# Norm sums as columns of tokens, and two merge groups moved behind the attention drain, in a kernel of two nets

## The chip, the cores and the metric

The kernel runs on 1 core of one Trainium2 chip. The metric is the device time of one execution in microseconds (us). The engines are named as the profile names them: PE (TensorE, matrix products), PEld (its weight loads), DVE (VectorE), ACT (ScalarE), POOL (GpSimd) and SP (SyncE, which here only issues transfers).

## The reference, cut to what matters

Two nets run one after the other on 512 tokens of 1024 channels in fp32. Each has two layers.

```
# first net, each of DEPTH = 2 layers
h = rms_norm(x, g_mix[l]);  proj = h @ w_in[l]
y_a, y_b, y_c = mla_mixer(...), dilated_mixer(...), neighbourhood_mixer(...)
gates = sigmoid(gate_logits)
merged = gates[0]*(y_a @ w_pa[l]) + gates[1]*(y_b @ w_pb[l]) + gates[2]*(y_c @ w_pc[l])
x = x + merged @ w_o[l]
x = x + (silu(rms_norm(x, g_ffn[l]) @ w1[l]) * (rms_norm(x, g_ffn[l]) @ w3[l])) @ w2[l]
...
x = rms_norm(x, g_final)
# second net, each of 2 layers
h = layer_norm(x) * (1 + scale) + shift          # scale, shift, gate from c @ w_ada[l] + b_ada[l]
proj = h @ w_in[l]
y = [attention | short convolution | fourier], each times silu(gate)
x = layer_norm(alpha * x + gate * (y @ w_out[l])) * ln_g[l] + ln_b[l]
```

## The kernel before

Channels lie on partitions: an activation is 8 tiles of 128 channels x 512 tokens. An fp32 product is made of three matmuls of halves (`mm3`, L267 to L271): hi x hi (L269), lo x hi (L270), hi x lo (L271). `weights` (L257 to L264) loads a weight tile `wst` by a transfer that SP issues; ACT makes its high half `whi` (L251), DVE its low half `wlo` (L252). A scheduler orders the instructions of each engine before the run, and each engine then goes through its own list in that order. SP's list holds nearly all weight loads and the loads and stores of `td`, a buffer in HBM. PSUM has banks named mm (3), S (2), O (1) and T (2).

**First net.** `branches` runs the groups of the attentions (scores L341, exponentials on ACT, transposes L365, value products L406, and the division at the end, L415 to L417 and L506 to L508) and weaves "fill" between them: products of the gates and of the branches that stand ready. The last stretch of fill is `first_products`: for each n of 8 a "merge group" of 42 matmuls, namely the gate of branch a (24), y_a @ w_pa (12, weights `wpa`) and y_b @ w_pb (6, weights `wpb`); the sum goes to `td[n]`. When the fill is used up, the last two attention groups still have to finish: that stretch is called the drain below. Behind it stands the loop over w_pc (12 matmuls for each n, which go to the banks S, T, O, mm by turns; it loads `td[16+n]` into a tile O and `td[n]` into a tile tmp), then the loop over w_o. The product y_c needs all of the last attention groups for its last two k-tiles of 128 only.

**Second net.** The work before it and between its layers has three passages in which a norm over channels stands between two stretches of matrix products. A sum over channels is a matmul of a 128x128 tile of ones with a 128x512 tile (`add_sum`, L1105), which gives the sum of all tokens on every partition:
- A, `centre` (L1107 to L1156): both norms (rms of the first net, layer norm of the second). POOL adds up the tiles for n < 7, and the sums of tile 7 are added on PE; `fold` (L1090) sums the modulation on PE in matmuls of one column; the square root is taken on ACT (L1176) and the reciprocal on DVE on 128x512 (L1185); then `less_mean` and `put_h` (L1266, L1267) make the input hh of the next products.
- B, between the layers (L1478 to the end of `second_layer`): POOL adds up x and its square (L1494, L1495), DVE x times the gain (L1489); then 5 sums, a pass over the 8 tiles (L1546 to L1550, 16 sums on PE), a fold, a reciprocal and `put_h`.
- C, the last norm (L1500 to L1533): the sums, then subtraction, a reciprocal in two halves, scaling and 8 output transfers.

Of the kernel before, what the change touches and what calls it, by code (L numbers as in the profile page):

```python
# [19 lines left out]
D = 1024  # L20
# [194 lines left out]
class _Net:  # L215
# [357 lines left out]
    def first_layer(self, l, acc, xsrc, emit_x):  # L573
        nc, a = self.nc, self.a
        with ExitStack() as lctx:
# [45 lines left out]
            def first_products(early):  # L621

                yh, yl = ys["a"]
                bh, bl = ([x[:, i] for i in range(2)] for x in (qk_tiles(), qk_tiles()))
                put = [load_split(4 + i, bh[i], bl[i]) for i in range(2)]
                yield from gates(len(todo))
                for f in put:
                    f()
                for n in range(8):
                    if n == 6:  # L630
                        early()
                    t = self.t(self.tp, "gate", (P, S), bufs=2)
                    yield from gate(0, n, t)
                    w = self.weights(a["wpa"][l, n])
                    pz = self.bank("mm")
                    for i in range(4):
                        o = slice(i * P, i * P + P)
                        self.mm3(pz, w[0][:, o], w[1][:, o], yh[:, i], yl[i], i == 0, i == 3)
                        yield 650
                    nc.vector.scalar_tensor_tensor(t, t, 1.0, pz, op0=ALU.add, op1=ALU.mult)  # L640
                    t1 = self.t(self.tp, "E", (P, S), bufs=3)
                    nc.sync.dma_start(out=t1, in_=td[8 + n])
                    w = self.weights(a["wpb"][l, n])
                    pz = self.bank("mm")
                    yield from self.dense_steps(pz, w, (bh, bl), range(2))
                    nc.vector.scalar_tensor_tensor(t1, t1, 1.0, pz, op0=ALU.add, op1=ALU.mult)
                    nc.gpsimd.tensor_tensor(t, t, t1, op=ALU.add)
                    nc.sync.dma_start(out=td[n], in_=t)
                    yield 0

            with ExitStack() as actx:
# [4 lines left out]
                              first_products, load_split, qk_tiles, qc)  # L656

# [115 lines left out]
    def branches(self, l, r, put_r, gates, first_outputs, first_products, load_split, qk_tiles, qc):  # L773
# [279 lines left out]
        fills[6] += 8 * 9100  # L1053
# [52 lines left out]

    def centre(self, n, x, state):  # L1107
# [21 lines left out]
        if 0 < n < 7:  # L1129
            for k, y in (("d", d), ("x", sq), ("q", dq)):  # L1130
                nc.gpsimd.tensor_tensor(state[k], state[k], y, op=ALU.add)
        if n == 6:
            self.pm, self.pv, self.px = (self.bank(t) for t in "SOT")
            self.add_sum(self.px, state["x"], True, False)
            self.add_sum(self.pm, state["d"], True, False)
            self.add_sum(self.pv, state["q"], True, False)
            self.root_table(sq)
        if n == 7:
            self.add_sum(self.px, sq, False, True)
            self.add_sum(self.pm, d, False, True)  # L1140
            at = self.add_sum(self.pv, dq, False, True)
            pg = self.bank("mm")
# [4 lines left out]
            m2, q = (self.t(self.tp, t, (P, S), bufs=2) for t in ("s", "xo"))  # L1147
            r = self.scale = self.fp.tile([P, S], F32, name="scale")
            nc.scalar.activation(m2, self.pm, AF.Square, scale=1.0 / D)
            nc.scalar.activation(self.mean, self.pm, AF.Copy, scale=1.0 / D)  # L1150
            nc.vector.tensor_scalar(q, self.px, 1.0 / D, EPS, op0=ALU.mult, op1=ALU.add)
            nc.vector.scalar_tensor_tensor(m2, q, LN_EPS, m2, op0=ALU.mult, op1=ALU.subtract)
# [59 lines left out]
    def second_net(self):  # L1212
        nc, a, tc = self.nc, self.a, self.tc
        with ExitStack() as ctx:
# [8 lines left out]
            sd = self.t(self.tp, "tmp", (P, S))  # L1223
            nc.scalar.activation(sd, self.px, AF.Sqrt, scale=1.0 / D, bias=self.eps)
            nc.vector.reciprocal(self.r0, sd)
# [18 lines left out]
            self.gb = cp.tile([P, 8], F32, name="gb")  # L1244
            nc.vector.tensor_tensor(self.gb, self.col("ln_g0", 0, 8), self.bcol, op=ALU.mult)
            b2 = self.t(cp, "rq", (P, 8), bufs=2)
            nc.vector.tensor_tensor(b2, self.bcol, self.bcol, op=ALU.mult)
            pb = self.bank("ms")
            nc.tensor.matmul(pb[:, 0:8], self.onef, b2, start=True, stop=True)
            self.bvar = cp.tile([P, 1], F32, name="bvar")  # L1250
            nc.vector.tensor_reduce(self.bvar, pb[:, 0:8], axis=AX.X, op=ALU.add)
            nc.vector.tensor_scalar(self.bvar, self.bvar, 1.0 / D, LN_EPS, op0=ALU.mult, op1=ALU.add)
# [20 lines left out]
    def second_layer(self, l, cp, chan, ind, ropex):  # L1273
# [77 lines left out]
        def transform(j):  # L1351
            fm = self.t(self.tp, "fm", (P, P), bufs=1)
# [98 lines left out]
        ax, aq, ag = (self.t(self.tp, "E", (P, S), bufs=3) for _ in range(3))  # L1451
# [5 lines left out]
        y, early, xg = (yh, yl), [], {}  # L1457
        if last:
            xgs = [x[:, i] for x in [self.t(cp, t, (P, 2, S)) for t in ("v2", "f2l", "f2h")] for i in range(2)]
            ng = self.t(cp, "rq", (P, 8), bufs=2)  # L1460
            nc.vector.tensor_scalar(ng, self.col(f"ln_g{l}", 0, 8), -1.0, None, op0=ALU.mult)
# [5 lines left out]
        for n in range(8):  # L1467
# [13 lines left out]
            if last and n not in (3, 5, 7):  # L1481
                xg[n] = xgs.pop()
                nc.scalar.activation(xg[n], x, AF.Copy, scale=self.col(f"ln_g{l}", n))
# [14 lines left out]
        px, pq = self.bank("S"), self.bank("O")  # L1498
        self.add_sum(px, ax, True, False)
        self.add_sum(pq, aq, True, False)  # L1500
        self.add_sum(px, xt[7], False, True)
        self.add_sum(pq, sq, False, True)
        m = self.mean_of(px)
        v = self.t(self.tp, "rs", (P, S), bufs=1)
        self.root_of(v, pq, self.squared_mean(px), ALU.subtract, self.eps_ln)
        if last:
            for n in range(8):

                x, g = xt[n], self.col(f"ln_g{l}", n)
                if n in (3, 5, 7):  # L1510
                    nc.gpsimd.tensor_tensor(x, x, m, op=ALU.subtract)
                    nc.scalar.activation(x, x, AF.Copy, scale=g)
                else:
                    with self.tc.issue_after(self.v_at) if n > 1 else ExitStack():
                        nc.vector.scalar_tensor_tensor(x, m, ng[:, n:n + 1], xg[n], op0=ALU.mult, op1=ALU.add)
            r = self.t(self.tp, "mu2", (P, S), bufs=1)
            at = None
            for c in (slice(0, S // 2), slice(S // 2, S)):
                with self.tc.issue_after(at) if at else ExitStack():
                    self.one_over(v[:, c], r[:, c])  # L1520
                for n in range(8):
                    x = xt[n][:, c]
                    if n in (3, 7):
                        nc.gpsimd.tensor_tensor(x, x, r[:, c], op=ALU.mult)
                    else:
                        at = nc.vector.tensor_tensor(x, x, r[:, c], op=ALU.mult).ins
                    if n in (4, 6):
                        nc.vector.tensor_scalar(x, x, self.col(f"ln_b{l}", n), None, op0=ALU.add)
                    else:
                        nc.scalar.activation(x, x, AF.Identity, bias=self.col(f"ln_b{l}", n))  # L1530
                    if n % 2:
                        dst = self.out[(n - 1) * P:(n + 1) * P, c].rearrange("(i p) s -> p i s", i=2)
                        nc.sync.dma_start(out=dst, in_=xp[n // 2][:, :, c])  # L1533
            return
# [3 lines left out]
        pg, pa, pb = self.bank("S"), self.bank("T"), self.bank("T")  # L1538
        self.add_sum(pg, ag, True, True)
        mg = self.mean_of(pg, "mu2")  # L1540
        nc.vector.scalar_tensor_tensor(mg, m, self.ngbar, mg, op0=ALU.mult, op1=ALU.add)
        col = lambda name, n: self.col(f"{name}{l}", n)
# [130 lines left out]
```

## Time and profile before

| | |
|---|---|
| time, median of 3 runs | 2413.41 us (2408.09 to 2414.17) |
| profiled execution, its own time | 2413.86 us |
| its span in the trace | 2412.1 us |
| PE busy | 2323.6 us (96%) |
| DVE busy | 1576.2 us (65%) |
| ACT busy | 1169.7 us (48%) |
| POOL busy | 707.0 us (29%) |
| granted clock of TensorE, mean | 0.984 |

The span is what the trace covers; 1.8 us of the execution's own time lie around it. A busy share is an average over the whole span: stretches in which PE waits have to be looked up one by one.

### The profile page before, as it was taken

The page shows a single profiled execution, that of the slowest core. Times are in us where ns is not written, and L with a number is a line of the kernel's source. Part 1 is how long each engine was busy: PE and PEld are TensorE (multiplying, and loading weights), DVE is VectorE, ACT ScalarE, POOL GpSimd, SP SyncE. Part 2 cuts the span into 40 slices and gives each one's busy share as a digit, 9 for nine tenths or more (in the row PEclk, how much of TensorE's full clock was granted, in tenths as well). Part 3 has the DMA queues.
Part 4 walks back from the last instruction along what each step waited for, and adds up shares of the span by engine and source line. Part 5 has one row for each costly group of instructions (what it writes and reads, how often), then busy time and mean ns, then how long its engine had stood idle before and what let it go on. Part 6 is the DMA issues. An engine that isn't in the chain of part 4 may idle for free. (4 is left out here: it accounts for less than half of the span.)

```text
span 2412.1 us, 31728 instructions
## 1 busy us (share of the span) xinstructions
PE 2323.6 (96%) x11356; PEld 1930.6 (80%) x11356; DVE 1576.2 (65%) x2367; ACT 1169.7 (48%) x2064; POOL 707.0 (29%) x773
## 2 busy tenths in 40 slices
PE   8999999989999999999999999999999899979995
PEld 6888887868888888888887878878877788758884
DVE  6878797765343334878698665876333867686766
ACT  5666685434222223666685444323232466346653
POOL 3225555332111001225366332111111221332215
PEclk9999999999999999999999999999999899989997
DMA  5455556555333344465466656875343432323222
GB/s 186 144 161 163 149 175 223 189 166 166 97 99 100 100 131 139 150 182 143 143 170 206 197 181 209 269 248 180 94 148 121 122 93 73 98 89 104 84 75 78
DMA packets 129709, 352.58 MB, mean 146 GB/s; under 512 B 20856, under 2 KB 28248, under 8 KB 129552
## 3 DMA queue, kind: packets, MB, share of 16 engines
q1 hardware_dynamic: 103760, 279.91, 36.0%
q0 software_dynamic: 25792, 70.65, 10.2%
q8 instruction: 89, 1.46, 0.2%
q14 instruction: 68, 0.56, 0.1%
HBM read 281.54 MB, written 41.66 MB: 134 GB/s over the span
## 5 line engine op out<-in xcount | busy, mean ns | idle before, releaser
L251 ACT ACTIVATE whi<-wst 128x1024 fp32r<-128x1024 f32 (+4 forms) x387 | 374.0, 967 | 614.4 <-PE mm L270 178.5
L252 DVE TENSOR_TENSOR wlo<-wst,whi 128x1024 fp32r<-128x1024 f32 (+4 forms) x387 | 481.7, 1245 | 255.5 <-ACT whi L251 255.1
L269 PE MATMUL mm<-hh,whi 128*128 128x512 f32 x1184 | 472.1, 399 | 0.5 <-ACT tmp L538 0.5
L271 PE MATMUL mm<-hh,wlo 128*128 128x512 f32 x1184 | 466.2, 394 | 0.9 <-DVE wlo L252 0.9
L270 PE MATMUL mm<-hl,whi 128*128 128x512 f32 x1184 | 466.6, 394 | 0.0
L271 PEld LDWEIGHTS mm<-hh,wlo 128*128 128x128 f32 x1184 | 223.5, 189 | 48.7 <-DVE wlo L252 1.8
L269 PEld LDWEIGHTS mm<-hh,whi 128*128 128x128 f32 x1184 | 223.8, 189 | 41.1 <-ACT tmp L538 0.7
L270 PEld LDWEIGHTS mm<-hl,whi 128*128 128x128 f32 x1184 | 223.8, 189 | 40.5 <-issue 0.2
L706 POOL TENSOR_TENSOR s<-s,rf 128x512 f32<-128x512 f32 x44 | 75.2, 1709 | 399.5 <-ACT s L705 399.5
L541 POOL DMA_DIRECT2D ry<-tmp x136 | 67.8, 505 | 188.7 <-ACT tmp L538 87.3
L365 PE MATMUL T<-ident,E 128*128 128x128 f32 x768 | 117.5, 273 | 4.1 <-ACT E L350 3.1
L251 ACT ACTIVATE ph<-T 128x512 fp32r<-128x512 f32 x160 | 94.8, 596 | 51.2 <-PE T L365 48.8
L365 PEld LDWEIGHTS T<-ident,E 128*128 128x128 f32 x768 | 93.8, 140 | 22.8 <-ACT E L350 3.9
L341 PE MATMUL S<-qk,qk 128*128 128x512 f32 (+2 forms) x512 | 106.6, 326 | 0.0
L252 DVE TENSOR_TENSOR pl<-T,ph 128x512 fp32r<-128x512 f32 x128 | 87.4, 684 | 27.1 <-ACT ph L251 26.5
L417 POOL TENSOR_TENSOR O<-O,ll 64x256 f32<-64x256 f32 x72 | 74.0, 1033 | 91.8 <-DVE O L416 83.5
L350 ACT ACTIVATE E<-E,stats 128x256 f32<-128x256 f32 (+1 forms) x160 | 72.9, 457 | 49.8 <-DVE stats L348 49.2
L303 POOL TENSOR_TENSOR tmp<-tmp,tmp 128x512 f32<-128x512 f32 x26 | 42.2, 1622 | 172.2 <-ACT tmp L299 168.5
L269 PE MATMUL S<-hh,whi 128*128 128x512 f32 x208 | 82.2, 395 | 6.1 <-ACT hh L254 6.1
L341 PEld LDWEIGHTS S<-qk,qk 128*128 128x128 f32 x512 | 79.6, 191 | 9.3 <-issue 0.3
L271 PE MATMUL S<-hh,wlo 128*128 128x512 f32 x208 | 81.6, 392 | 0.9 <-DVE wlo L252 0.9
L270 PE MATMUL S<-hl,whi 128*128 128x512 f32 x208 | 81.9, 394 | 0.0
(649 smaller groups left out, 5503.3 us busy)
## 6 DMA issues: line engine op xcount, KB each, us to landing
wst<-win SPq DMA_DIRECT2D x153, 512.0 KB, 3.8
wst<-w SPq DMA_DIRECT2D x120, 512.0 KB, 3.6
mw<-wada SPq DMA_DIRECT2D x48, 512.0 KB, 4.3
td<-gate SPq DMA_DIRECT2D x48, 256.0 KB, 3.6
qk<-qk POOLq DMA_DIRECT2D x40, 256.0 KB, 4.2
ry<-tmp POOLq DMA_DIRECT2D x136, 64.0 KB, 3.9
V<-vd POOLq DMA_DIRECT2D x16, 512.0 KB, 5.5
wst<-wo SPq DMA_DIRECT2D x16, 512.0 KB, 4.0
```

What stands on the lines that cost most here:

```text
L251: nc.scalar.activation(hi, src, AF.Copy)
L252: nc.vector.tensor_tensor(lo, src, hi.bitcast(F32), op=ALU.subtract)
L269: mm(out, ah, bh, start=start, stop=False, **kw)
L270: mm(out, ah, bl, start=False, stop=False, **kw)
L271: mm(out, al, bh, start=False, stop=stop, **kw)
L303: self.nc.gpsimd.tensor_tensor(new, acc, sq, op=ALU.add)
L341: nc.tensor.matmul(sp[:, i * nk:(i + 1) * nk], a, b, start=n == 0, stop=n == len(ops) - 1)
L350: nc.scalar.activation(e[:, sl], e[:, sl], AF.Exp, scale=-1.0, bias=m, accum_out=d)
L365: nc.tensor.transpose(tp[:, i * P:(i + 1) * P], e[:, i * P:(i + 1) * P], self.ident)
L417: self.summed = nc.gpsimd.tensor_tensor(dst, dst, lo, op=ALU.add)
L541: nc.gpsimd.dma_start(out=y[r:r + 32], in_=f[r ^ 32:(r ^ 32) + 32])
L706: nc.gpsimd.tensor_tensor(s, s, r, op=ALU.mult)
```

## The change

1. **Merge groups.** `first_products` makes the groups n = 0 to 5 as fill; the groups 6 and 7 are called after `branches`, that is behind the attention's last groups in the program's text. The budget of the last fill goes from 8 to 6 groups, and `early_outputs` starts at n = 5 instead of 6. This holds in both layers.
2. **Passage A.** The three sums are made with the data as the weights of the matmul and a column of ones as its moving side (`token_sums`: 4 matmuls for a tile), so that a statistic is a 128x4 tile (token on the partition). The square root, the reciprocal and the small arithmetic are done on that. `spread_tokens` brings a statistic back to 128x512: four diagonal 128x128 tiles (ACT or DVE) and one matmul with ones. `r0`, a factor used later, is made in the same way.
3. **Passage B.** The sums over x and its square, with up to four weights at once (`lw`), are made by `token_sums` behind each tile of the output product. The additions on POOL (L1494, L1495 for this layer), the products L1489 on DVE, the 16 sums and the 128x512 reciprocal go; four statistics are spread, and the tiles are then normed from PSUM.
4. **Passage C.** In the same way, with two spreads; then for each n one operation on DVE, one on ACT and one addition (DVE, or POOL for n = 1, 3, 5) and an output transfer.
5. The tile `fm` of `transform` comes from another ring.

```diff
@@ first_layer
+            def first_products(early):
...
-                for n in range(8):
-                    if n == 6:
+                for n in range(6):
+                    if n == 5:
                         early()
-                    t = self.t(self.tp, "gate", (P, S), bufs=2)
-                    yield from gate(0, n, t)
...
+                    yield from first_product(n)
+
+            def first_product(n):
+                yh, yl = ys["a"]
+                bh, bl = ys["b"]
+                t = self.t(self.tp, "gate", (P, S), bufs=2)
+                yield from gate(0, n, t)
+                w = self.weights(a["wpa"][l, n])
...
                 self.branches(l, r, lambda: self.inv_root(self.ones_sum(acc), D, self.eps, r), gates, first_outputs,
                               first_products, load_split, qk_tiles, qc)
+
+                for n in (6, 7):
+                    for _ in first_product(n):
+                        pass
@@ branches
-        fills[6] += 8 * 9100
+        fills[6] += 6 * 9100
@@ new
+    def token_sums(self, ps, x, w, first, last):
+
+
+        for b in range(4):
+            at = self.nc.tensor.matmul(ps[:, b], x[:, b * P:(b + 1) * P], w, start=first and b == 0, stop=last and b == 3)
+        return at
+
+    def spread_tokens(self, ps, c, act=False):
+
+        dg = self.t(self.tp, "tmp", (P, 4, P))
+        for b in range(4):
+            if act:
+                self.nc.scalar.activation(dg[:, b], self.ident, AF.Copy, scale=c[:, b:b + 1])
+            else:
+                self.nc.vector.tensor_scalar(dg[:, b], self.ident, c[:, b:b + 1], None, op0=ALU.mult)
+        return self.nc.tensor.matmul(ps, self.onef, dg.rearrange("p b q -> p (b q)"), start=True, stop=True)
@@ centre (passage A)
-            self.add_sum(self.px, sq, False, True)
-            self.add_sum(self.pm, d, False, True)
-            at = self.add_sum(self.pv, dq, False, True)
...
+            for i, y in enumerate((d, dq, sq)):
+                at = self.token_sums(self.pst[:, :, i:i + 1], y, one, False, i == 2)
...
+            (m, q, x2), z = self.token_stats(self.pst, 3)
+            pm, self.scale = self.bank("mm"), self.bank("mm")
+            self.spread_tokens(pm, m, act=True)
...
-            self.root_of(r, self.pv, m2, ALU.add, 0.0)
-            self.one_over(r, r)
...
+            nc.scalar.activation(z[2], z[0], AF.Sqrt)
+            nc.vector.reciprocal(z[3], z[2])
+            self.spread_tokens(self.scale, z[3])
@@ second_layer, output products (passages B and C)
-            if not last:
-                g = self.col(f"ln_g{l}", n)
-                if n == 0:
-                    nc.vector.tensor_scalar(ag, x, g, None, op0=ALU.mult)
-                else:
-                    nc.vector.scalar_tensor_tensor(ag, x, g, ag, op0=ALU.mult, op1=ALU.add)
-            if n == 0:
+                self.token_sums(pst[:, :, 0:4], x, self.lw[:, 0:4, n], n == 0, False)
+                at = self.token_sums(pst[:, :, 4:6], sq, self.lw[:, 2:4, n], False, n == 7)
+            elif n == 0:
@@ second_layer, between the layers (passage B)
+        self.spread_tokens(pm, m, act=True)
+        mu = self.t(self.tp, "mu", (P, S), bufs=1)
+        nc.scalar.activation(mu, pm, AF.Copy)
...
+        self.spread_tokens(pg, z[2])
...
+        self.spread_tokens(pv, z[1])
+        nc.vector.reciprocal(z[7], z[6])
+        self.spread_tokens(pr, z[7])
...
         for n in range(8):
-            at = self.put_h(l + 1, n, xt[n], r2)
-        with late(at):
-            self.one_over(v, self.r0)
+            if n not in (3, 5, 7):
+                tt(xt[n], xt[n], pm, op=ALU.subtract)
+            stt(xt[n], xt[n], col("ln_g", n), pg, op0=ALU.mult, op1=ALU.subtract)
+            if n < 5:
+                stt(xt[n], pv, self.bcol[:, n:n + 1], xt[n], op0=ALU.mult, op1=ALU.add)
...
+            at = self.put_h(l + 1, n, xt[n], pr)
+        p0 = self.bank("mm")
+        self.spread_tokens(p0, z[8], act=True)
+        nc.scalar.activation(self.r0, p0, AF.Copy)
@@ second_layer, last norm (passage C)
+            self.spread_tokens(pr, z[2])
+            self.spread_tokens(pm, z[3], act=True)
             for n in range(8):
...
+                x, u = xt[n], self.t(self.tp, "tmp", (P, S))
+                nc.vector.scalar_tensor_tensor(x, x, self.col(f"ln_g{l}", n), pr, op0=ALU.mult, op1=ALU.mult)
+                nc.scalar.activation(u, pm, AF.Identity, scale=ng[:, n:n + 1], bias=self.col(f"ln_b{l}", n))
+                (nc.gpsimd if n in (1, 3, 5) else nc.vector).tensor_tensor(x, x, u, op=ALU.add)
+                nc.sync.dma_start(out=self.out[n * P:(n + 1) * P], in_=x)
```

The first place is PE's list at the drain of layer 0. In it mm_5095 is the last merge product of the fill, T_5105 the transposes and O_5124 the value product of an attention group, and S_5158 is the first product of the w_pc loop. Before, these rows stand there:

```order
L271 MATMUL mm_5095<-qk_4154,wlo_5091 128x512
L365 MATMUL T_5105<-ident,E_4987 128x128 x4
L506 MATMUL T_5116<-ident,rd_5113 8x128
L406 MATMUL O_5124<-pl_5037,V_3839 128x256 x4
L269 MATMUL S_5158<-qk_4913,whi_5160 128x512
```

In the changed kernel the same transposes are T_4961, the value product is O_4980, and mm_5005 is the gate product (24 matmuls) of merge group 6:

```order
L271 MATMUL mm_4951<-qk_4154,wlo_4947 128x512
L365 MATMUL T_4961<-ident,E_4873 128x128 x4
L506 MATMUL T_4972<-ident,rd_4969 8x128
L269 MATMUL mm_5005<-hh,whi_5007 128x512
L270 MATMUL mm_5005<-hl,whi_5007 128x512
...
L406 MATMUL O_4980<-pl_4899,V_3839 128x256 x4
L271 MATMUL mm_5005<-hh,wlo_5008 128x512
```

What moved: between the transposes and the w_pc loop now stand the 84 matmuls of the groups 6 and 7, and the value products stand among them (O_4980 behind 8 of mm_5005, the last one, O_4990, behind 33 of the 84).

The second place is SP's list in the same stretch (O tiles are the loads of `td[16+n]`, wst of wpc are the weights of the w_pc loop, and `td_174<-gate` stores a merged group). Before:

```order
L664 DMA O_5240<-td_174 128x512
L263 DMA wst_5215<-wpc 128x512
L664 DMA O_5268<-td_174 128x512
L664 DMA O_5296<-td_174 128x512
L782 DMA cosr_9540<-ropeB 128x512
L782 DMA sinr_9542<-ropeB 128x512
L263 DMA wst_5243<-wpc 128x512
L263 DMA wst_5271<-wpc 128x512
L648 DMA td_174<-gate_5015 128x512
```

In the changed kernel:

```order
L673 DMA O_5240<-td_174 128x512
L673 DMA O_5268<-td_174 128x512
L263 DMA wst_5215<-wpc 128x512
L673 DMA O_5296<-td_174 128x512
L673 DMA O_5324<-td_174 128x512
L791 DMA cosr_9540<-ropeB 128x512
L791 DMA sinr_9542<-ropeB 128x512
L263 DMA wst_5243<-wpc 128x512
L263 DMA wst_5271<-wpc 128x512
L653 DMA td_174<-gate_5076 128x512
```

What moved: a second load into an O tile stands ahead of the weights wst_5215. The ring of O tiles also holds low halves of y_a, which the products with wpa of group 7 read last, and that group now stands behind the drain on PE; so the O loads, and the weights of w_pc behind them in SP's list, are free to go only after it.

The third place is PE's list in passage B. In both O, S, T and mm are banks; dft1l is tile x of n = 6 or 7, tmp its square or (L1131) the diagonal tiles, f2h to v2 the modulation's sums, and S_18571 or S_18647 the first product of the next layer. Before:

```order
L1105 MATMUL T_18420<-tmp_18453,onef 128x512
L1105 MATMUL T_18420<-tmp_18458,onef 128x512
L1105 MATMUL T_18420<-tmp_18463,onef 128x512
L1094 MATMUL mm_18466<-onef,f2h_18084 128x1 x8
L1094 MATMUL mm_18466<-onef,f2l_18085 128x1 x8
L1094 MATMUL mm_18466<-onef,v_3430_18086 128x1 x8
L269 MATMUL S_18571<-whi_18576,hh 128x384
```

In the changed kernel:

```order
L271 MATMUL mm_18445<-y2h_16463,wlo_18448 128x512
L1120 MATMUL O_18122<-lw,dft1l_18121 128x4 x4
L1120 MATMUL O_18122<-lw,tmp_18477 128x2 x4
L1103 MATMUL S_18487<-onef,f2h_18123 128x1 x8
L1103 MATMUL S_18487<-onef,f2l_18124 128x1 x8
L1103 MATMUL S_18487<-onef,v_3430_18125 128x1 x8
L1131 MATMUL mm_18512<-tmp_18519,onef 128x512
L1131 MATMUL mm_18513<-tmp_18532,onef 128x512
L1131 MATMUL mm_18514<-tmp_18550,onef 128x512
L1131 MATMUL T_18515<-tmp_18557,onef 128x512
L269 MATMUL S_18647<-whi_18652,hh 128x384
```

What moved: the 21 wide sums that stood ahead of the fold are gone; 14 of 16 calls of `token_sums` stand within the output products ahead of these rows (six of them in one run, L1120 x4 each), the last two and the fold stand ahead of the four spreads, and on DVE 17 operations of 128x512 stand ahead of the first `put_h`.

## Rows read from the trace of the kernel before

**Rows 1.** Windows: busy us (instructions) of each engine, PE's clock, DMA share, GB/s.

```profile
500.00:600.00 100.00, 92.16 (x390) 74.57 (x389) 59.00 (x65) 41.61 (x58) 32.05 (x23) 0.97 0.53 172
1800.00:1900.00 100.00, 92.45 (x409) 76.05 (x409) 53.28 (x73) 32.73 (x46) 19.62 (x15) 0.95 0.40 125
2100.00:2200.00 100.00, 86.44 (x378) 67.28 (x377) 85.73 (x107) 44.80 (x76) 35.36 (x31) 0.90 0.34 108
2300.00:2400.00 100.00, 85.51 (x404) 67.30 (x402) 66.71 (x96) 47.33 (x85) 34.08 (x28) 0.93 0.20 66
```

**Rows 2.** PE's waits: releaser, us in total, times, longest.

```profile
PE S L1105 <- POOL E L1494: 13.9, 2, 10.3
PE S L269 <- ACT hh L1267: 8.9, 2, 6.2
PE O L406 <- DVE O L416: 4.9, 2, 2.7
PE S L269 <- ACT qk L251: 4.7, 2, 2.7
```

**Rows 3.** Timeline of PE, drain of layer 0: start, us, instruction, [idle before <-releaser].

```profile
499.24 0.40 PE L269 MATMUL S<-qk,whi 128*128 128x512 f32 x1
...
506.85 0.50 PE L269 MATMUL O<-qk,whi 128*128 128x512 f32 x1 [1.75 <-DVE O L416]
...
511.91 0.80 PE L269 MATMUL S<-qk,whi 128*128 128x512 f32 x1 [2.71 <-ACT qk L251]
...
515.58 0.39 PE L269 MATMUL mm<-qk,whi 128*128 128x512 f32 x1
515.80 0.40 PE L270 MATMUL mm<-qk,whi 128*128 128x512 f32 x1
...
524.45 0.50 PE L269 MATMUL T<-qk,whi 128*128 128x512 f32 x1 [1.99 <-ACT whi L251]
...
531.20 0.39 PE L269 MATMUL mm<-qk,whi 128*128 128x512 f32 x1
```

**Rows 4.** Timeline of PE, drain of layer 1.

```profile
1418.94 0.40 PE L269 MATMUL S<-qk,whi 128*128 128x512 f32 x1
...
1433.64 0.39 PE L269 MATMUL mm<-qk,whi 128*128 128x512 f32 x1
...
1448.59 0.39 PE L269 MATMUL S<-V,whi 128*128 128x512 f32 x1
```

**Rows 5.** Timeline of DVE and of PE in passage A.

```profile
1867.30 0.75 DVE L1125 SCALAR_TENSOR_TENSOR u<-xn,cols,shift 128x512 f32<-128x512 f32 x1
...
1869.81 1.02 PE L1105 MATMUL O<-tmp,onef 128*128 128x512 f32 x2
1870.67 1.84 PE L1094 MATMUL mm<-onef,macc 128*128 128x1 f32 x16
...
1878.91 0.69 PE L269 MATMUL S<-whi,hh 128*128 128x384 f32 x1 [6.17 <-ACT hh L1267]
```

**Rows 6.** Timeline of PE and of DVE in passage B.

```profile
2111.35 0.40 PE L271 MATMUL mm<-y2h,wlo 128*128 128x512 f32 x1
2122.00 2.07 PE L1105 MATMUL S<-E,onef 128*128 128x512 f32 x2 [10.25 <-POOL E L1494]
...
2147.39 3.35 DVE L1185 RECIPROCAL mu<-mu 128x512 f32<-128x512 f32 x1 [0.70 <-ACT mu L1176]
...
2152.65 0.69 PE L269 MATMUL S<-whi,hh 128*128 128x384 f32 x1 [2.76 <-ACT hh L1267]
```

**Rows 7.** Groups by shape of matmuls with few columns: ns min/median/max, first and last start.

```profile
L1094 PE MATMUL mm<-onef,v x16: 250/352/353, 2146.5 to 2149.5; 128*128 128x1 f32 x16
L1343 PE MATMUL T<-ind,tmp x8: 165/251/251, 2191.1 to 2191.8; 128*128 128x2 f32 x8
```

**Rows 8.** Groups by shape of DVE and ACT operations, same columns.

```profile
L1478 DVE SCALAR_TENSOR_TENSOR dft1l<-mm,mod,RD x2: 739/742/744, 2119.3 to 2120.7; 128x512 f32<-128x512 f32 x2
L1489 DVE SCALAR_TENSOR_TENSOR E<-dft0l,cols,E x2: 1408/1594/1779, 2102.4 to 2105.9; 128x512 f32<-128x512 f32 x2
L251 ACT ACTIVATE cmh<-T x8: 259/282/308, 1893.5 to 2206.3; 128x128 fp32r<-128x128 f32 x8
L309 DVE RECIPROCAL rq<-tmp x8: 193/203/203, 1921.4 to 2285.5; 128x8 f32<-128x8 f32 x8
```

**Rows 9.** Timeline of PE and of DVE in passage C.

```profile
2383.84 2.08 PE L1105 MATMUL S<-E,onef 128*128 128x512 f32 x2 [3.69 <-POOL E L1494]
2385.71 1.91 PE L1105 MATMUL S<-dft1l,onef 128*128 128x512 f32 x2
...
2405.02 0.34 DVE L1528 TENSOR_SCALAR dft1l<-dft1l,cols 128x256 f32<-128x256 f32 x1
```

More of the change, by code (lines that the diff above doesn't have):

```diff
@@ new lines, in first_products @@
+                    yield from first_product(n)
[5 more added lines that the diff above has]
+                w = self.weights(a["wpa"][l, n])
+                pz = self.bank("mm")
+                for i in range(4):
+                    o = slice(i * P, i * P + P)
+                    self.mm3(pz, w[0][:, o], w[1][:, o], yh[:, i], yl[i], i == 0, i == 3)
+                    yield 650
+                nc.vector.scalar_tensor_tensor(t, t, 1.0, pz, op0=ALU.add, op1=ALU.mult)
+                t1 = self.t(self.tp, "E", (P, S), bufs=3)
+                nc.sync.dma_start(out=t1, in_=td[8 + n])
+                w = self.weights(a["wpb"][l, n])
+                pz = self.bank("mm")
+                yield from self.dense_steps(pz, w, (bh, bl), range(2))
+                nc.vector.scalar_tensor_tensor(t1, t1, 1.0, pz, op0=ALU.add, op1=ALU.mult)
+                nc.gpsimd.tensor_tensor(t, t, t1, op=ALU.add)
+                nc.sync.dma_start(out=td[n], in_=t)
+                yield 0
@@ L1131, in centre @@
                 nc.gpsimd.tensor_tensor(state[k], state[k], y, op=ALU.add)
+        one = self.onef[:, 0:1]
         if n == 6:
[L1133 to L1136, printed above, removed]
+            self.pst = self.bank("O")[:, 0:12].rearrange("p (b i) -> p b i", b=4)
+            for i, k in enumerate("dqx"):
+                self.token_sums(self.pst[:, :, i:i + 1], state[k], one, i == 0, False)
@@ L1155, in centre @@
+            nc.scalar.activation(z[2], z[0], AF.Sqrt)
+            nc.vector.reciprocal(z[3], z[2])
+            self.spread_tokens(self.scale, z[3])
+            nc.scalar.activation(z[4], z[1], AF.Sqrt)
+            self.r0c = self.fp.tile([P, 4], F32, name="r0c")
+            self.r_at = nc.vector.reciprocal(self.r0c, z[4]).ins
+            self.v_at = self.r_at
             with self.tc.issue_after(self.r_at):
@@ L1450, in second_layer @@
         xp, xt = self.x_tiles()
-        ax, aq, ag = (self.t(self.tp, "E", (P, S), bufs=3) for _ in range(3))
+        if last:
+            ax, aq = (self.t(self.tp, "E", (P, S), bufs=3) for _ in range(2))
+        else:
+            pst = self.bank("O")[:, 0:24].rearrange("p (b i) -> p b i", b=4)
         if not last:
@@ L1456, in second_layer @@
                 nc.sync.dma_start(out=parts[i], in_=self.md[i])
-        y, early, xg = (yh, yl), [], {}
+        y, early = (yh, yl), []
         if last:
-            xgs = [x[:, i] for x in [self.t(cp, t, (P, 2, S)) for t in ("v2", "f2l", "f2h")] for i in range(2)]
             ng = self.t(cp, "rq", (P, 8), bufs=2)
@@ L1560, in second_layer @@
-        for n in order:
-            nc.vector.scalar_tensor_tensor(xt[n], xt[n], col("ln_g", n), mg, op0=ALU.mult, op1=ALU.subtract)
-        def whole(n):
-            nc.vector.scalar_tensor_tensor(xt[n], v, self.bcol[:, n:n + 1], xt[n], op0=ALU.mult, op1=ALU.add)
-        for n in (7, 6, 5):
-            bv = self.t(self.tp, "tmp", (P, S))
-            nc.scalar.activation(bv, v, AF.Copy, scale=self.bcol[:, n:n + 1])
-            nc.gpsimd.tensor_tensor(xt[n], xt[n], bv, op=ALU.add)
-        for n in range(5):
-            whole(n)
@@ L1572, in second_layer @@
[L1572 to L1575 removed]
+        pm, pg, pv, pr = (self.bank(t) for t in ("mm", "mm", "mm", "T"))
+        (xgb, xg1, m, xg2, x2, x2g2), z = self.token_stats(pst, 6)
+        self.spread_tokens(pm, m, act=True)
+        mu = self.t(self.tp, "mu", (P, S), bufs=1)
+        nc.scalar.activation(mu, pm, AF.Copy)
+        tt, stt = nc.vector.tensor_tensor, nc.vector.scalar_tensor_tensor
```

164 lines of the change are left out of this document (68 added, 96 removed).

## The prediction

> **What bounds the kernel now.** I began with busy time by stretches of 100 us. PE is at 100% in most of them, so the kernel is bound by PE, and only the stretches where PE falls short can give time: around 500, 1800, 2100 and 2300 us [rows 1]. Then the list of PE's waits: the longest are on the sums of passages B and C, which wait for POOL's additions, on the first hh behind A and B, and on the division at the end of the attention (L416) and what follows it [rows 2]. All of them lie in the three passages and the two drains that the change touches. The timelines of those places give the prices.
>
> **Drains (part 1).** In layer 0 the w_pc loop starts at 499.24 and reaches the first matmul of n = 3 at 515.58 [rows 3]. Between lie 36 matmuls of the loop. Dense ones follow each other at about 0.23 us (515.58 to 515.80), which makes 8.3 us, and value products 0.5: 8.8 of 16.34 us are work, 7.5 are lost, in waits for L416 (1.75) and for the split of y_c (2.71), and in matmuls at half clock behind them. The next 48 (n = 3 to 6) take 15.6 us to 531.20 where 11.0 are work: 4.6 lost, 1.99 of it in a wait for weights of w_pc [rows 3] and most of the rest at half clock behind it. In layer 1 the same 36 take 14.70 (5.9 lost) and the next 60 take 14.95 (1.2 lost) [rows 4]. Together 13.4 us in the drains and 5.8 behind them, 19.2 in all.
>
> After, 84 matmuls of groups 6 and 7 stand there, 84 x 0.23 = 19.3 us, more than the 14.7 to 16.3 us that the chain of division, transfer and split takes now; so what waits for the chain can wait behind work. The total of matmuls does not change. What stays: value products that come due early (O_4980 behind 8 matmuls, 1.8 us; O_4990 behind 33, 7.6 us, and it was due 5.2 us behind 499.24), the split of group 7's sum, and the weights of w_pc, which come later in SP's list. I take 4 us a layer as left, near the mean of the 4.6 and 1.2 that weights and the like cost now plus one wait of 1.75; from 1 (only the 1.2 of layer 1) to 6.5 (that 4.6 and the 1.75). Gain 19.2 - 8 = 11.2, from 6.2 to 17.2.
>
> **Passage A (part 2).** Now: the last difference u starts at 1867.30, and the first product behind the passage at 1878.91 [rows 5]. After: u ends 1868.05, its square (0.6) 1868.7, its token sum is 4 matmuls in two rows each. The nearest row is L1343: 8 rows of two columns from 2191.1 to 2191.8, 0.1 us each, so 0.8 a call at full clock; the other bound is L1094 on v, 16 rows in 3.0 us, 0.19 each or 1.5 a call [rows 7]. So statistics are there at 1869.5 to 1870.2, copied (0.28, the ACT row of 128x128) at 1870.5. Fold, 1.84 us [rows 5], and the first spread come on PE meanwhile. Small operations on 128x4: six of about 0.2 on three engines (a reciprocal of 128x8 is 0.2 [rows 8]; the 3.35 us one on 128x512 [rows 6] goes), four diagonal tiles of 0.28: 2.4 us and hops of 0.1, so 1873.4. One spread is a sum of two rows: 0.86 us (1869.81 to 1870.67 [rows 5]) at full clock or 1.87 (2383.84 to 2385.71 [rows 9]) at half. Then put_h (0.74 [rows 8]) and hh (about as long) and a hop: 1876.0 to 1877.4. Half clock is nearer, since PE has small work only for 5 us: 1877.2, gain 1.7 (0.5 to 2.9). The spread for r0 falls into dense work, 0.86 on PE where the old reciprocal lay on DVE and cost PE nothing: -0.9. A: +0.8.
>
> **Passage B (part 3).** Now PE stops at 2111.35, begins the sums at 2122.00 and the next layer at 2152.65 [rows 6]: 41.3 us. The 10.25 us are DVE's and POOL's lag: L1489 takes 1.4 to 1.8 us on two operands in SBUF while POOL works, L1478 with an operand in PSUM 0.74 [rows 8]. Without L1489 and POOL's additions DVE has some 10 us less there (8 of about 1.3), so PE sets the pace. The Trainium skill names a cause (GPSIMD Engine Reference, section Specifications): POOL's SBUF interface is shared with DVE, and DVE operations with two SBUF inputs contend for it. The trace agrees: 1.8 us against 0.74.
>
> After: 14 of the 16 calls of token_sums stand within the dense work, 14 x 0.8 = 11.2 us, so it ends at 2122.6; x of tile 7, its square and two more calls bring 2124.9 at full clock, 2127 with the run of six and the last ones half at the slow price. Then the fold: 48 rows x 0.1 = 4.8, or 48 x 0.19 = 9.1 [rows 7]; the spread for pm 0.86 or 1.87. pm is there at 2130.6 to 2138. On DVE small operations and diagonal tiles (14 x 0.17, 12 x 0.28, 3 x 0.2) with hops take about 7.5 us from 2125.2, so DVE is free at 2132.7. Then 17 operations of 0.7 stand ahead of the first put_h: 12 us. With put_h and hh, 1.5: the first product at 2146.2 to 2151.5, and 2153.5 if every spread that DVE needs is late as well. Against 2152.65: +6.4 to -0.9. The fold of before, in the same position, fell to 0.19 a row on its last third [rows 7]; I take the first product at 2150.6, +2.0, less 0.9 for r0's spread. B: +1.1.
>
> **Passage C (part 4).** Now the first sum starts at 2383.84, 3.69 late and at half clock, and the last operation of DVE ends at 2405.36 [rows 9]. After, POOL's additions stay. Four calls at 1.5: 2389.9 (before, four sums at 1.87 make 2391.3); small operations and diagonals 3.2; spread 1.87: 2395.0. DVE then has 8 of 0.74 and 5 additions of 0.7 (1.4 beside POOL's three): 9.4 to 12.9, so 2404.4 to 2407.9 for the last; at full clock 2.5 earlier. I take 2404.4. C: +1.0 (-2.5 to +3.5).
>
> **Part 5** changes a ring only. In the opening of each second-net layer the first score product (L341) stands 26 places later in PE's list: all of PE's work there is the same, so I price it at nothing; if cover is missing behind it, it is one wait like the 1.95 to 2.76 above.
>
> **Sum.** 11.2 + 0.8 + 1.1 + 1.0 = 14.1 on the profiled execution's own 2413.86, which is 0.45 over the median: 2399.8, for the median about 2399.3; I say 2399.
>
> **A rule against the change.** What the trace shows first: the granted clock falls when PE has little to do, the fold's rows go from 0.1 to 0.19 us, and the first product behind B takes 0.69 for 384 columns, half clock [rows 6, 7]. The Trainium skill (TensorE: Matmul & The Clock Gate, Part 1: The HAM clock gate) says that the throttled clock is the default and sustained activity lifts it. By that rule alone all small matmuls and the first products behind them would run at 1.2 GHz, which is rival a.
>
> **Rivals.**
> *a, the small matmuls cost the clock.* 16 calls of one to four columns among the dense products of B, the fold and all spreads at half clock: B at -0.9 - 0.9, and the dense products behind the run of six calls slow by some 1.5; A +0.5 - 0.9, C -2.5. For it: the fold's last third. Against: the first 32 rows of that fold ran at 0.1. Passages -6.2 in place of +2.9: 2413.86 - 11.2 + 6.2 = 2408.9; with C at 0, 2406.4.
> *b, slower: the weights of w_pc wait in SP's list.* The loads into O tiles stand ahead of wst for n = 2 to 7 and can go only when y_a @ w_pa of group 7 has read its tiles. For it: SP goes in order, and one late weight costs 1.99 now [rows 3]. Against: 18 matmuls (4.1 us) and n = 0, 1 (5.5 us) stand between. Behind it PE went on at half clock, and the whole stretch lost 4.6. If six weights in each layer are late, at 2.8 each (the wait, and half of what the clock cost behind it), 33.6 us come in against 19.2 that the drains and the weights cost now and 2.9 from the passages: 2413.86 - 22.1 + 33.6 = 2425.4. It decides from 22.1 / 12 = 1.8 us each, clock and wait together.
> *c, the stall moves.* Two merge groups less in the fill bring the last attention groups closer together, and value products wait ahead of merge work: 6.5 us left per layer, gain 6.2, passages 0: 2407.7.
> *d, all at full clock:* 17.2 + 2.0 + 5.5 + 3.5 = 28.2: 2385.7.
>
> **How the numbers follow.** Forecast 0.52 (its own range 2394 to 2405), a 0.17, b 0.09, c 0.13, d 0.09. A measurement of this kernel can tell about 0.3%, 7.2 us, from no change: faster is below 2406.2. To faster go 0.51 of the forecast, all of d, 0.08 of a and 0.05 of c, 0.73; slower is b, 0.08 above 2420.6; the rest, 0.19, is the same. The range 2387 to 2411 leaves out b and about half of d, and takes in the low ends of c and a.
>
> **What the changed profile would show.** Drains: between the last transposes and the w_pc loop some 19 us of mm products without a gap, waits for L416 and for the split of y_c gone from PE's list, no L269 over 1 us late on wst of w_pc. A: first product 1.7 us sooner after u; no 3.3 us reciprocal. B: no wait for POOL, from the end of the dense work to the next layer 28 us (2122.6 to 2150.6). C: last DVE operation some 20.5 us behind the first sum. I am wrong if waits for whi of w_pc behind the drains sum up to more than 10 us, or if dense products among the token sums show half clock.

## The result, and the profile after

The changed kernel takes 2437.69 us (median of 4 runs, 2431.88 to 2440.90), the kernel before 2413.14 beside it: ratio 1.0109 (95% interval 1.0094 to 1.0124). It is slower by 24.6 us; 2399 with a range up to 2411 was forecast. The profiled execution took 2439.26 us, its span is 2437.5.

The page of the changed kernel, span and busy time:

```profile
span 2437.5 us, 32025 instructions
PE 2366.5 (97%) x11522; PEld 1959.8 (80%) x11522; DVE 1547.4 (63%) x2386; ACT 1167.8 (48%) x2063; POOL 679.4 (28%) x754
PEclk9999999999999999999999999999998999889997
```

PE is busy 43 us longer than before (2366.5 against 2323.6) and stands idle 17 us less (71.0 of the span against 88.5). The windows of 100 us, with the columns of [rows 1], and one more from 600 to 700:

```profile
500.00:600.00 100.00, 99.60 (x433) 80.56 (x432) 60.87 (x67) 41.55 (x56) 29.37 (x18) 1.00 0.57 187
600.00:700.00 100.00, 100.00 (x431) 80.49 (x430) 39.95 (x45) 28.94 (x36) 16.13 (x9) 1.00 0.29 94
1800.00:1900.00 100.00, 94.71 (x414) 78.32 (x414) 46.58 (x74) 30.88 (x47) 20.39 (x15) 0.90 0.36 112
2100.00:2200.00 100.00, 90.20 (x431) 78.32 (x430) 57.69 (x111) 33.80 (x64) 10.25 (x10) 0.80 0.31 101
2300.00:2400.00 100.00, 97.82 (x501) 80.92 (x500) 69.57 (x110) 51.25 (x88) 23.83 (x26) 1.00 0.25 82
```

The stretch 500 to 600 is nearly full, as forecast for the drain. But from 600 to 700, in a feed-forward that the change does not touch, PE is busy all the time at full clock and gets through 431 matmuls, where the same stretch of a kernel with the same instruction order and other addresses (run pad2048, below) has 443. The longest waits of PE in the changed kernel:

```profile
PE S L269 <- ACT hh L1312: 11.5, 2, 9.0
PE T L365 <- ACT E L350: 6.2, 3, 3.0
PE S L269 <- ACT hh L254: 6.1, 1, 6.1
PE O L406 <- DVE O L416: 3.8, 2, 1.9
PE O L1120 <- POOL E L1535: 3.7, 1, 3.7
PE mm L269 <- ACT y2h L254: 3.2, 2, 1.9
PE S L1131 <- DVE tmp L1130: 2.2, 1, 2.2
PE mm L269 <- DVE dpl L252: 1.9, 2, 0.9
```

Against [rows 2]: the 10.3 us for POOL in passage B and the waits for the split of y_c are gone; new are waits for y2h and dpl, two tiles that are split into halves inside the second net's layers. Three things are to be explained: slower matmuls everywhere, new waits in places that were priced at nothing, and the passages.

Timeline of PE in the changed kernel at 700 us, where nothing waits (start, us, instruction):

```profile
700.18 0.40 PE L269 MATMUL T<-hh,whi 128*128 128x512 f32 x1
700.42 0.40 PE L270 MATMUL T<-hl,whi 128*128 128x512 f32 x1
700.65 0.40 PE L271 MATMUL T<-hh,wlo 128*128 128x512 f32 x1
700.88 0.40 PE L269 MATMUL mm<-hh,whi 128*128 128x512 f32 x1
```

They follow each other after 0.233 us; in the kernel before, 441 matmuls between 600 and 700 us have a mean distance of 0.2267. In the trace of before nearly all dense products that run undisturbed have one of these two distances. Which one it is goes with the moving tile (the operand of the matmul that is not the weights): hh, hl, V and gh0 have 0.227, and gh1, nq and y2h 0.233. (gh0 and gh1 are the inputs of w2 in the two layers of the first net, nq that of w_pa, y2h a high half in the second net.) In the changed kernel hh, hl and gh1 have 0.233, V and gh0 0.227. That pointed to where the tiles lie. The built programs say it (bytes within a partition):

```
                          before    changed   distance of its products, us
hh                         18944      18944
tile behind hl and accf   scale 2048  r0c 16 (takes 32)
whi (first of its ring)    55808      53792
hh - whi, modulo 512           0         480   0.227 -> 0.233
V - whi, modulo 512            0           0   0.227 -> 0.227
gh1 - whi, modulo 512         32         288   0.233 -> 0.233
```

r0c, a 128x4 tile, took the place of scale in a pool that lasts for the whole kernel, so the weights behind it moved by 2016 bytes against hh and hl. V and gh0 kept their distance from the weights modulo 512.

### The profile page after: what moved, and what is told of

Same layout as the page of the kernel before. It is cut to its first block, busy times and chain, and to the rows that moved or that the text cites. A ratio compares the mean times of both kernels' runs of the same rounds, so it can differ in the third digit from the quotient of the medians.

```text
span 2437.5 us, 32025 instructions
## 1 busy us (share of the span) xinstructions
PE 2366.5 (97%) x11522; PEld 1959.8 (80%) x11522; DVE 1547.4 (63%) x2386; ACT 1167.8 (48%) x2063; POOL 679.4 (28%) x754
```

## The experiments

Ratios are to the kernel before, measured beside each run.

**Where the tiles lie.** Theory 1: a dense product follows the one before 6.6 ns later when its moving tile and its weights do not lie alike modulo some power of two. Rival: the order, or the phase between weight loads and matmuls.

Run pad64, 64 bytes for r0c:

```diff
-            self.r0c = self.fp.tile([P, 4], F32, name="r0c")
+            self.r0c = self.fp.tile([P, 16], F32, name="r0c")[:, 0:4]
```

> The changed kernel with the 16-byte tile r0c made 64 bytes long (128x16, of which the first 4 columns are used); every instruction and its order stay. Theory 1 (placement): r0c takes 32 bytes where a tile of 2048 stood, so the rings of weights whi and wlo lie 32 bytes off a multiple of 64 while hh and hl lie on one, and a dense matmul of such a pair follows the one before after 233 ns and not after 227. With 64 bytes the products of hh are back at 227 ns, and about 24 us go (the difference in spacing by stretches of 100 us, times the matmuls in them): 2413 us (2409 to 2417). Rival (order): the slower spacing comes from the order or phase in which weight loads and matmuls now stand; nothing moves: 2434 to 2440.

2442.44 us, ratio 1.0129 (1.0116 to 1.0143): nothing was won. Either the power is above 64 or theory 1 falls; the next two decide.

Run before32, the kernel before with its weights moved by 32 bytes:

```diff
-            r = self.scale = self.fp.tile([P, S], F32, name="scale")
+            r = self.scale = self.fp.tile([P, S + 8], F32, name="scale")[:, 0:S]
...
-            self.bvar = cp.tile([P, 1], F32, name="bvar")
+            self.bvar = small[:, 2:3]
```

> The kernel before with 32 more bytes behind the tile scale, and one small tile of the second net put into another so that memory suffices; every instruction and its order stay. Theory 1: the weight rings move to 32 modulo 64, the products of hh and hl go from 227 to 233 ns, those of y2h get faster (both sides at 32): plus 24 less 2, 2435 us (2430 to 2440). Rival (order): 2413 (2408 to 2416).

2432.64 us, ratio 1.0090 (1.0076 to 1.0104): 21.5 us slower by 32 bytes alone (y2h, at 448 from the weights, did not gain). The second part of the edit makes room; it stands in the next run too, and costs nothing there. Run allshift, hh and all behind it moved together:

```diff
-            self.cols = cst.tile([P, self.ncols], F32, name="cols")
+            self.cols = cst.tile([P, self.ncols + 8], F32, name="cols")[:, 0:self.ncols]
```

> The kernel before with 32 bytes more ahead of hh, so that hh, hl, the weight rings and all behind them move by 32 together. Theory 1 in the form that a pair counts (moving tile and weights must lie alike modulo 64): products of hh stay at 227 ns, those of y2h get faster by 2 us: 2411 us (2407 to 2415). Rival form (the weights' or the moving tile's own address must be a multiple of 64): all dense products at 233 ns, 2435 or more.

2412.94 us, ratio 1.0009 (1.0000 to 1.0018). So it is the pair and not an address by itself. The window from 600 to 700 us of before32 and then of allshift:

```profile
600.00:700.00 100.00, 100.00 (x430) 80.53 (x429) 39.95 (x45) 28.95 (x36) 16.13 (x9) 1.00 0.30 93
```

```profile
600.00:700.00 100.00, 100.00 (x443) 82.81 (x442) 39.93 (x45) 28.98 (x37) 16.13 (x9) 1.00 0.32 100
```

430 against 443 matmuls in the same 100 us. Two more paddings of r0c in the changed kernel settle the size. Run pad2048 (tile of 128x512, all as in the kernel before) and run pad128 (128x32):

> The changed kernel with r0c as long as the tile whose place it took (2048 bytes), so that the weight rings lie at the addresses of the kernel before; instructions and their order stay. 64 bytes changed nothing, so the rule of 64 is wrong; theory 1 now: hh and the weights must lie alike modulo 128, 256 or 512 (the weights of one matmul start at steps of 512 bytes). All three are met here: products of hh at 227 ns, 24 us less, 2414 us (2410 to 2418). Rival (order or phase): 2437 to 2443.

> The same with 128 bytes. Modulus 128: products of hh at 227 ns, 2414 us. Modulus 256 or 512: 233 ns, 2438 to 2442.

pad2048: 2416.55 us, ratio 1.0015 (1.0006 to 1.0024); pad128: 2440.98 (2 runs), ratio 1.0114 (1.0097 to 1.0132). With an order that is the same row by row on all engines, 21.1 us go or stay with the address alone (18 to 27 by the two ratios and their intervals). With 128 bytes the kernel is as slow as with 32. pad2048 between 600 and 700 us:

```profile
600.00:700.00 100.00, 100.00 (x443) 82.84 (x442) 41.86 (x48) 29.72 (x38) 16.12 (x9) 1.00 0.30 95
```

**The merge groups alone** (part 1 put into the kernel before; the diff is that of the change):

> The kernel before with part 1 alone: merge groups 6 and 7 behind the drain. Placement stays as before. The trace of the changed kernel reaches the w_o loops 6.5 and 3.2 us sooner in each layer although its products are slower by some 4 us in each: theory 1 expects 16 to 17 us of gain, 2396 to 2398. By the term of the prediction 11.2: 2402. Rival (late weights of w_pc, as in the prediction's b): 2413 or more.

2392.97 us, ratio 0.9931 (0.9917 to 0.9944): 18.2 us faster. Its trace shows no wait of PE at all in layer 0 from the last value product (487.45) to the first product with w_o (521.42), and the granted clock is 1.00 there; nor does that of the changed kernel show a wait in its drains:

```profile
487.45 0.65 PE L406 MATMUL O<-ph,V 128*128 128x256 f32 x4
521.42 0.39 PE L269 MATMUL S<-V,whi 128*128 128x512 f32 x1
```

Before, that product with w_o started at 533.92. It is 12.5 us sooner, and in layer 1 the same place (1448.59 before [rows 4], 1429.89 in merges) is 18.7 us sooner.

**The passages alone** (parts 2 to 5 with r0c of 2048 bytes; part 5 is in it too):

> Parts 2 to 4 alone (all 8 merge groups in the fill as before), with r0c of 2048 bytes so that the placement is that of before. From the trace of the changed kernel, slower products taken off: A +3 us, B +6.6, C +0.4, the stretch between B and C +5: about 15 us slower than before, 2426 (2420 to 2431). By the prediction's terms: 2.9 faster, 2408.

2431.66 us, ratio 1.0078 (1.0056 to 1.0099). 19.4 us slower (13.5 to 24 by the interval; the six runs scatter from 2421 to 2439), more than the 15 that the trace of the changed kernel had given and far from the forecast's 2.9 faster.

**Passage B put back** (noB: pad2048 with the old sums, fold, pass and reciprocals between the layers):

> The changed kernel with r0c of 2048 bytes and passage B as before (sums on POOL, DVE and with ones on PE, reciprocals on 128x512); merge groups, A and C as changed. If B with what follows it costs what the trace shows (6.6 to 12 us): 2403 (2400 to 2408), against pad2048's 2414. If A and C carry the loss: 2410 or more.

2411.03 us, ratio 0.9996 (0.9987 to 1.0005): 5.5 less than pad2048, so B alone costs 5.5 (some 1.5 to 7.5 by the two intervals). But the stretch behind it, from the second layer's first product to its output products, still took 175.6 us where merges takes 170.8, with B's old code in both. Something besides the passages cost time there: part 5 is still in noB.

**Part 5.** Run fmtmp is the kernel before with one line changed; run noBfm is noB with that line as before (and r0c of 512 bytes):

```diff
-            fm = self.t(self.tp, "fm", (P, P), bufs=1)
+            fm = self.t(self.tp, "tmp", (P, P))
```

> The kernel before with part 5 alone (tile fm from the ring tmp). The stretches from A to the output products and from B to those of the second layer are 5 us longer in the kernels with parts 2 to 5 than in the run merges, also where B is as before. If part 5 is what does it: 2419 to 2423. If the sums of A and the spread for r0 do: 2412.

> The run noB (B as before, merge groups, A and C as changed) with fm in its own ring again, and r0c 512 bytes long, so that the weights keep their place modulo 512. If part 5 costs the 5 us in each of two stretches: 2400. If not: 2411. Products of hh at 227 ns in both.

fmtmp: 2424.26 us, ratio 1.0054 (1.0039 to 1.0069), 12.8 us slower. noBfm: 2399.99, ratio 0.9951 (0.9936 to 0.9966), 11.0 faster than noB, and the stretch of 175.6 us takes 170.2. The addresses are not it: the dense products keep the distances of before in fmtmp (hh 0.227, y2h 0.233). PE is idle 9.4 us more there than before (97.9 against 88.5) and busy 2.1 more. PE's list of waits has these among others, of which the list of before has none among its longest:

```profile
PE mm L269 <- DVE dpl L252: 2.6, 3, 0.9
PE T L365 <- ACT E L358: 2.5, 2, 1.3
PE mm L269 <- ACT y2h L254: 2.4, 2, 1.2
PE mm L269 <- ACT f2h L251: 1.8, 1, 1.8
```

fm is zeroed on DVE and loaded by SP at the opening of each second-net layer. From the ring tmp it comes later: PE's product L1359, DVE's cml and SP's loads of fm are written behind other work, and some 1400 places of PE's list of matmuls hold another one than before. The waits are small and many; which of the moved rows causes which was not tried.

**Both side effects taken back** (clean: the changed kernel with r0c of 512 bytes and fm in its own ring):

> The changed kernel with both side effects taken back: r0c made 512 bytes long (weights in place modulo 512) and fm in its own ring, so that merge groups and passages A, B and C alone are left of the change. If the parts add up (merge groups -18, A and C together +7, B +5.5, from the runs merges, noBfm, noB and pad2048): 2406 (2402 to 2410). By the prediction's sum, which left placement and part 5 out: 2399. If something else of the change still costs: 2412 or more.

2407.50 us, ratio 0.9981 (0.9970 to 0.9991). That is within 2 us of the 2406 that the parts add up to, and what is left of the change is 4.1 us faster than before: 18.2 from the merge groups, less about 14 that the three passages cost.

**A version that beats both** (merges512: merge groups alone, with gh1 and gl1 on the weights' place modulo 512, and nq 256 from it):

```diff
-            r = gp.tile([P, S], F32, name=f"rf{l}")
+            r = gp.tile([P, S + (120 if l == DEPTH - 1 else 0)], F32, name=f"rf{l}")[:, 0:S]
...
-        c = self.t(self.cp, tag, (P, 4))
+        c = self.t(self.cp, tag, (P, 48 if tag == "rc" else 4))[:, 0:4]
```

> The kernel before with the merge groups (part 1) and two paddings: gh1, gl1 of the first net's second feed-forward move to a multiple of 512 bytes from the weights (they lie 32 off in the kernel before, and their 528 products take 233 ns), nq of the branch a moves from 96 to 256 off. The order of instructions is that of the run merges. Modulus 256: nq's products go to 227 as well, 5 us less than merges, 2388. Modulus 512: only gh1's, 3.5 us less, 2389.5. If placement were not the cause: 2393 as merges.

2387.97 us, ratio 0.9903 (0.9887 to 0.9920), the fastest here. The products of gh1 take 123.00 us where they took 126.38, as forecast. Those of nq fell from a mean distance of 233.8 ns to 229, the level of hh's products in that stretch (229.4): so 256 seems enough, but in a stretch where other work stands between, this is not settled.

## Why the prediction was wrong

The prediction added up four gains, 14.1 us, and 24.6 us of loss came out. The step that decided it is the one that gives every dense product "about 0.23 us" on both sides and then says that "the total of matmuls does not change": it left out that the change moves the weights, and with that the distance of the products went from 0.227 to 0.233 us, +21.1 us. Two more steps failed beside it: part 5 "at nothing" (+11.0) and the passages at +2.9 of gain (12 to 14 of loss). Only the drains gained, and more than forecast.

**The drains** were right in mechanism and too small: 11.2 us (6.2 to 17.2) against 18.2. "I take 4 us a layer as left" is what failed: of the 19.2 us that the step counted as lost, the trace of merges wins back 18.7 (12.5 in layer 0, 6.2 in layer 1). No wait is left, PE stays at full clock (1.00 in the drains of merges, 0.89 to 0.90 in those of before), and the late weights of [rows 3] are gone with the drain.

**Rival b** did not happen: the loads behind the O tiles in SP's list came in time, no wait for whi of w_pc remains.

**Passage A** was forecast to gain 0.8 and lost 3.3: from the last dense product to the first one behind it took 12.82 us (1866.09 to 1878.91) and takes 16.13. The last dense product before the change, and then the timeline of PE in the changed kernel:

```profile
1866.09 0.39 PE L271 MATMUL mm<-gh,wlo 128*128 128x512 f32 x1
```

```profile
1868.69 0.39 PE L271 MATMUL mm<-gh,wlo 128*128 128x512 f32 x1
...
1870.78 1.05 PE L1120 MATMUL O<-onef,u 128*128 128x1 f32 x8 [1.57 <-DVE u L1158]
1871.69 3.14 PE L1120 MATMUL O<-onef,tmp 128*128 128x1 f32 x16
1874.70 3.55 PE L1103 MATMUL S<-onef,macc 128*128 128x1 f32 x16
1878.11 0.63 PE L1292 MATMUL T<-lw,onef 128*128 128x40 f32 x2
1878.54 3.76 PE L1131 MATMUL mm<-tmp,onef 128*128 128x512 f32 x4
1884.82 0.45 PE L269 MATMUL S<-whi,hh 128*128 128x384 f32 x1 [2.53 <-ACT hh L1312]
```

The step counted one call of token_sums behind u; three stand there, and the fold takes 3.4 us at half clock (0.50 from 1875 to 1878 us), not 1.84, and stands ahead of both spreads. Small operations on DVE were cheap, as forecast; PE's row of small matmuls became the chain. (The step's low end of 0.5 does not follow from its own 1877.4 either, which gives 1.5.)

A cost some more ahead of the passage, which the step has nowhere: the three calls for the tiles n < 7 stand in one run among the last dense products of the first net (1858.16 to 1860.75), and behind them the granted clock falls in this trace, to 0.61 on the mean of 4 us:

```profile
1858.00:1861.00 3.00, 3.00 (x27) 2.96 (x26) 0.00 (x0) 0.00 (x0) 0.00 (x0) 1.00 0.30 116
1861.00:1865.00 4.00, 4.00 (x12) 3.09 (x12) 0.11 (x1) 0.84 (x1) 0.00 (x0) 0.61 0.00 0
```

From their first to their last, the products of gh1 take 128.0 us here, in pad2048 and in noBfm, but 126.5 in noB and clean, which have the same calls, and 126.4 before. Why the clock falls in some of these traces and not in others is not shown. In the trace of clean the passage itself takes 14.2 us.

**Passage B.** From its last dense product to the next layer it takes 27.7 us (2141.20 to 2168.94); "28 us" was forecast, 41.3 were before. What failed is "14 x 0.8 = 11.2 us" for the calls within the dense products: that stretch, from its first to its last dense product, grew from 57.4 (2053.94 to 2111.35) to 77.6 us, in pad2048 to 75.9. In pad2048 the 14 calls take 14.7 us and the dense products among them some 3.6 more. The first dense product before, then the changed kernel's windows, then its first dense product, the run of six calls (its last two shown), fold and spreads:

```profile
2053.94 0.40 PE L269 MATMUL mm<-y2h,whi 128*128 128x512 f32 x1
```

```profile
2116.00:2122.00 6.00, 6.00 (x38) 6.00 (x38) 0.69 (x1) 0.00 (x0) 0.00 (x0) 0.66 0.01 3
2122.00:2128.00 6.00, 6.00 (x18) 5.03 (x19) 1.31 (x2) 1.31 (x2) 0.00 (x0) 0.50 0.00 0
```

```profile
2063.62 0.39 PE L269 MATMUL mm<-y2h,whi 128*128 128x512 f32 x1
...
2119.91 1.85 PE L1120 MATMUL O<-lw,dft1h 128*128 128x4 f32 x8
2121.61 1.85 PE L1120 MATMUL O<-lw,tmp 128*128 128x2 f32 x8
...
2141.20 0.48 PE L271 MATMUL mm<-y2h,wlo 128*128 128x512 f32 x1
...
2144.33 2.75 PE L1103 MATMUL S<-onef,f2h 128*128 128x1 f32 x16
2146.94 3.55 PE L1103 MATMUL S<-onef,f2l 128*128 128x1 f32 x16
2150.36 3.55 PE L1103 MATMUL S<-onef,v 128*128 128x1 f32 x16
2153.77 5.35 PE L1131 MATMUL mm<-tmp,onef 128*128 128x512 f32 x6
2158.96 1.02 PE L1131 MATMUL T<-tmp,onef 128*128 128x512 f32 x2
...
2168.94 0.69 PE L269 MATMUL S<-whi,hh 128*128 128x384 f32 x1 [8.96 <-ACT hh L1312]
```

Over the 6 us of the run the granted clock is 0.66 on the mean, in the 6 us of dense products behind it 0.50 (that is 1.2 GHz), and the calls take up to 1.7 us each; the fold is at half clock from its second third on (3.4 us for 16 rows against 2.6 for its first 16), and so are three of the four spreads (1.7 us each; the last takes 1.0). That is rival a, put at 0.17, and its sign, "dense products among the token sums show half clock", came true. For the dense products it was 3.6 us, not 1.5. The rule of the Trainium skill cited in the prediction (TensorE: Matmul & The Clock Gate, Part 1: The HAM clock gate) says that the low clock is the default and activity lifts it. Whether the trace agrees turns on what counts as activity, which no run here shows: by the profile PE is busy in all of these rows (6.00 of 6.00 us), and it loses the clock all the same.

**Passage C** was forecast at 1.0 less and is 0.4 more (32.32 and 32.73 us from the last dense product to the end). The first sum starts 4.07 us behind the last dense product, as it did, since POOL's additions stayed; the chain on DVE ended 21.2 us behind the first sum (20.5 forecast, 21.5 before), and the end came 7.4 us behind it (6.7 before). The last dense product and the first sum after, and DVE's last operation:

```profile
2404.75 0.39 PE L271 MATMUL mm<-y2h,wlo 128*128 128x512 f32 x1
2408.82 3.58 PE L1120 MATMUL O<-onef,E 128*128 128x1 f32 x16 [3.67 <-POOL E L1535]
...
2428.75 1.28 DVE L1560 TENSOR_TENSOR dft1l<-dft1l,tmp 128x512 f32<-128x512 f32 x2
```

The step's half clock for the calls was right: the four take 6.8 us, 6 were forecast.

**Part 5** was priced "at nothing", with at most one wait of 2.8 as the other bound: it cost 11.0 to 12.8 us. The order showed the rows moved; the error was to hold a stretch for safe because PE's work there stays the same. The waits of fmtmp are on DVE and ACT, which hand PE its operands there.

**The largest part, 21.1 of 24.6 us, was in no term**: the prediction prices instructions, and not where their operands lie. That two distances exist could be read in the trace of before (gh1 and y2h at 0.233, hh at 0.227); they were taken for one number, 0.23. That addresses decide which one it is could not be read there: it took the runs.

The sum from the runs: addresses +21.1, merge groups -18.2, part 5 +11.0, B +5.5, A with C +7.0 (noBfm against merges, medians from two sets of runs), together +26.4 against 24.6 measured. This sum closes by the way it is made, each term being the difference of two neighbours in one row of runs from the kernel before to the changed one; the 1.8 us between are the scatter of before from session to session, and each term is sure to some 3 to 5 us only (A with C from 0 to 10, where the traces give 3.3 + 0.4 and the 1.6 ahead of A). What checks it from outside is before32 (+21.5 for addresses alone), fmtmp (+12.8 for part 5 alone) and clean. The run passages fits worse: 19.4, where part 5, A, B and C give 23.5, the upper end of its interval.

## What to carry to other kernels

When a change adds, drops or resizes a tile in a pool that lives long, compare the addresses of weights and moving tiles of the dense products before and after: 32 bytes cost 0.9% here. Make a tiny tile as long as the one that it replaces (pad2048) or a whole 512 bytes long (clean), or put it where nothing big is allocated behind it (not tried here). A sum over channels by many small matmuls saves DVE and POOL, but a run of them cost PE its clock here, and the products behind it ran at half clock; dense work, like the merge groups, filled the drain without that.

## What the runs showed of the hardware

Back-to-back fp32r matmuls of 512 columns, each with new weights, follow each other after 226.7 ns when the moving tile and the weights lie alike modulo 512 bytes (hh in before, allshift and pad2048). When the moving tile's address less that of the weights is 32, 96, 224, 288, 448 or 480 modulo 512, it is about 233.3 ns (gh1, nq, y2h and hh in before, pad64, before32, noBfm and the changed kernel); at 384 it is 232.4 (hh in pad128), and at 64 some 230.5 on the mean of a scatter from 226 to 234 (products with hh as the weights in pad64). All of this is at full granted clock. The matmul's own recorded time is 389 and 395 ns, the weight load is 188 in both. Moving both tiles together changes nothing (allshift). Why the two sides meet is not shown by any run here.
